# PSUM banks for the early up tiles and the gate map of a PEER layer: a second tag for every other tile

## The chip, the cores and the metric

The kernel runs on one core of one Trainium2 chip. The metric is the device time of one execution in microseconds, from three runs of the kernel before, and one further execution that the hardware profiler recorded. The engines are TensorE (PE in the rows, its weight loads PEld), VectorE (DVE), ScalarE (ACT), GpSimd (POOL) and SyncE (SP, which issues most DMAs). Each has a queue of its own and works its instructions in the order in which they stand there.

## The reference, cut to what matters

One decoder layer on 1024 tokens of width 1024. Two mixers (a gated linear recurrence and a state-space scan) come first; the part that the change touches is the PEER layer behind them, a mixture of 16,384 single-neuron experts. Each token scores 2 x 128 keys for each of 8 heads, takes 16 of the 128 x 128 pairs per head, and sums gelu(h . u) times a gate times v over its 128 experts:

```python
def block(hb):
    qh = (hb @ w_q).reshape(tb, PEER_HEADS, 2, PEER_HALF)
    s1 = jnp.einsum('thd,nd->thn', qh[:, :, 0], keys1)
    s2 = jnp.einsum('thd,nd->thn', qh[:, :, 1], keys2)
    v1, i1 = lax.top_k(s1, PEER_TOPK)
    v2, i2 = lax.top_k(s2, PEER_TOPK)
...
    gates = jax.nn.softmax(best.astype(jnp.float32), axis=-1).astype(hb.dtype)
    act = jax.nn.gelu(jnp.einsum('td,thkd->thk', hb, u_tab[eidx]), approximate=False)
    return jnp.einsum('thk,thkd->td', gates * act, v_tab[eidx])
```

## The kernel before, in words

The tokens are split. For the first 384 the kernel gathers the rows of u and v that each token needs, one indirect DMA of 128 rows (one per token) at a time (`gather`, L957; dot products on VectorE at L982, weighted sums at L998). For the other 640 (`ND`) it computes densely: for each of 128 groups of 128 experts (a group is called an expert e in the code, and here) it multiplies the tile of u with all 640 tokens, applies GELU, multiplies with a map of gates, and multiplies the result with v.

The stage that the change touches stands between the mixers and the dense loop. It holds three things at once.

- `choose` (L895 to L951) on VectorE picks the experts of four blocks of 128 tokens.
- `gate_map` (L1011 to L1060) turns the picks of a block into a dense map, in steps of 8 tokens, 16 steps to a block, 80 in all. A step makes three one-hot tiles on VectorE (`oB` L1043, `oA` L1044, `oH` L1045), eight products `oL` on ScalarE (L1047), sixteen 128x128 matmuls on TensorE (L1051, L1052) into two PSUM tiles `pg` of four tokens each, and two copies of each tile on ScalarE (`Gs`, L1054). Both `pg` tiles have the tag `s5`, with two banks. The products `oL` and the one-hot tiles have three buffers each. The maps go to DRAM (`gd`, L1060).
- The early up tiles (L1352 to L1355): for 64 of the 128 experts the up product is made ahead of the dense loop and stored in DRAM (`sd`). `up` (L1076) loads 512 KB of u as two `raw` tiles, splits each into a high and a low part (`wload`, L308: a cast on ScalarE at L255, a subtraction on VectorE at L256), and makes two halves of 320 tokens. A half is 24 matmuls of 128x320 (L1087) into one PSUM tile with the tag `mm`, two banks, and a GELU on ScalarE (L1089).

PSUM has eight banks, and the kernel gives two to each of four tags: `mm`, `hg`, `s5` and `tr`. Before this stage `hg` holds tiles of the recurrence's heads and `tr` holds transposes; in the stage `tr` is used for the three transposes at the head of each gate-map block (L1026). In the dense loop the tags `hg`, `s5` and `tr` hold the sums over v (`banks`, L1111).

The order of work on each engine is not the order of the code. The program is built with a scheduler (the flag `schedule_with_timeline_sim` at the end of the file), which takes an instruction when its inputs and its buffer are free by its own model of the chip, and writes one fixed order for each engine. So the number of banks enters the order itself. The gathers on POOL are tied to marks: `gather` may not be issued before a certain weight split or matmul of the stage (L961 to L967).

Of the kernel before, what the change touches and what calls it, by code (L numbers as in the profile page):

```python
# [10 lines left out]
F32 = mybir.dt.float32  # L11
# [11 lines left out]
P = 128  # L23
# [3 lines left out]
BANK = 512  # L27
# [7 lines left out]
NSB = ND // 2  # L35
# [54 lines left out]
def hymba_kernel(  # L90
# [26 lines left out]
    def T(pool, shape, dt, tag, bufs=None):  # L117
        return pool.tile(shape, dt, name=f"{tag}_{next(cnt)}", tag=tag, bufs=bufs)
# [5 lines left out]
    def bc(ap, axis, n):  # L124
        a = ap.unsqueeze(axis)
        shape = list(a.shape)
        shape[axis] = n
        return a.to_broadcast(shape)
# [7 lines left out]
    ps = ctx.enter_context(tc.tile_pool(name="ps", bufs=2, space=bass.MemoryType.PSUM))  # L136
# [171 lines left out]
    def wload(src, nk):  # L308
        res = []
        for k0 in range(0, nk, KH):  # L310
            raw = T(wp, [P, KH * P], F32, "raw", bufs=NRAW)
            nc.sync.dma_start(raw, src[:, k0 * P : (k0 + KH) * P])
            w2 = T(wp, [P, 2, KH * P], F32R, "w2", bufs=NW2)
            marks[phase[0]].append(split(w2[:, 0, :], w2[:, 1, :], raw))
            res.append(w2)
        return res
# [694 lines left out]
    def gate_map(gm, blk):  # L1011
        ei = T(gm, [P, HK], I32, "dei")
        nc.sync.dma_start(ei, eid[blk])
        gf = T(gm, [P, HK], F32, "dgt")
        nc.sync.dma_start(gf, gtd[blk])
        sel = []
        for n, (op, c) in enumerate(((ALU.logical_shift_right, 7), (ALU.bitwise_and, NK - 1))):
            t = T(gm, [P, HK], I32, "seli")
            TS(t, ei, c, None, op)
            tf = T(gm, [P, HK], F32, f"self{n}")  # L1020
            nc.vector.tensor_copy(tf, t)
            sel.append(tf)
        sel.append(gf)
        pt = T(ps, [P, BANK], F32, "tr", bufs=2)
        for n, t in enumerate(sel):
            nc.tensor.transpose(pt[:, n * P : (n + 1) * P], t, ident)  # L1026
        sT = T(gm, [P, 3, P], F16, "selT", bufs=2)
        nc.scalar.copy(sT[:, 0:2, :], pt[:, 0 : 2 * P].rearrange("p (n t) -> p n t", n=2))
        gs = T(gm, [P, P], F32, "gsel")
        nc.scalar.mul(gs, pt[:, 2 * P : 3 * P], GSC)  # L1030
        nc.scalar.copy(sT[:, 2, :], gs)
        sL = T(gm, [P, P], F32, "self0")
        TT(sL, gs, sT[:, 2, :], ALU.subtract)  # L1033
        for g in range(P // TG):
            gq = [T(gm, [P, NI, TG], F32, "Gs", bufs=4) for _ in range(2)]
            for o8 in range(0, TG, OT):
                t8 = g * TG + o8
                col = lambda n: bc(sT[:, n, t8 : t8 + OT].rearrange("p (q r) -> p q r", r=2), 2, P)
                one = lambda tag: T(gm, [P, OT // 2, P, 2], F16, tag, bufs=3)
                A, B, Ah = one("oA"), one("oB"), one("oH")  # L1040
                Al = T(gm, [P, OT, P], F16, "oL", bufs=3)
                at = lambda t, i: t[:, i // 2, :, i % 2]
                TT(B, iotar, col(1), ALU.is_equal)  # L1043
                TT(A, iotar, col(0), ALU.is_equal)  # L1044
                TT(Ah, A, col(2), ALU.mult)  # L1045
                for i in range(OT):
                    nc.scalar.mul(Al[:, i], at(A, i), sL[:, t8 + i : t8 + i + 1])  # L1047
                for o4 in range(0, OT, 4):
                    pg = T(ps, [P, 4, P], F32, "s5", bufs=2)
                    for i in range(o4, o4 + 4):  # L1050
                        nc.tensor.matmul(pg[:, i - o4, :], at(B, i), at(Ah, i), start=True, stop=False)  # L1051
                        nc.tensor.matmul(pg[:, i - o4, :], at(B, i), Al[:, i], start=False, stop=True)  # L1052
                    for c in range(2):
                        nc.scalar.mul(  # L1054
                            gq[c][:, :, o8 + o4 : o8 + o4 + 4],
                            pg[:, :, c * NI : (c + 1) * NI].rearrange("p t i -> p i t"),
                            1.0 / GSC,
                        )
            for c in range(2):
                nc.sync.dma_start(gd[(blk * P - T0D) // TG + g, :, c * NI : (c + 1) * NI, :], gq[c])  # L1060

    def dense_in(du, gm):
        h2T = []
        for k in range(KD):
            t = T(du, [P, 2, ND], F32R, "h2T", bufs=KD)
            r = T(gm, [P, ND], F32, "S", bufs=3)
            nc.scalar.dma_start(r, h2s[k])
            split(t[:, 0, :], t[:, 1, :], r)
            h2T.append(t)
        return h2T  # L1070
# [2 lines left out]

    early = [i * NK // SPN for i in range(SPN)]

    def up(h2T, e, g):  # L1076

        w2 = wload(u_t[e], KD)
        for sb in range(2):
            cs_ = slice(sb * NSB, (sb + 1) * NSB)  # L1080
            pt = T(ps, [P, BANK], F32, "mm", bufs=2)[:, :NSB]
            n = 0
            for k in range(KD):
                wk = w2[k // KH]
                kc = slice((k % KH) * P, (k % KH + 1) * P)
                for i, j in ((0, 0), (0, 1), (1, 0)):
                    nc.tensor.matmul(pt, wk[:, i, kc], h2T[k][:, j, cs_], start=(n == 0), stop=(n == 3 * KD - 1))  # L1087
                    n += 1
            ACT(g[:, cs_], pt, AF.Gelu)  # L1089

    def dense(dp, dq, h2T):
# [4 lines left out]
        def gate(e):  # L1096
            if e % IG == 0:
                gtile[0] = T(dq, [P, NTG, IG, TG], F32, "gt", bufs=2)
                nc.sync.dma_start(gtile[0], gd[:, :, e : e + IG, :].rearrange("n p i t -> p n i t"))
            g = T(dp, [P, ND], F32, "S", bufs=NS)  # L1100
            if e in early:
                nc.sync.dma_start(g, sd[early.index(e)])
            else:
                up(h2T, e, g)
            gv = g.rearrange("p (n t) -> p n t", t=TG)
            TT(gv, gv, gtile[0][:, :, e % IG, :], ALU.mult)  # L1106
            w = ws[e] = T(dp, [P, 2, ND], F32R, "W", bufs=NW)
            split(w[:, 0, :], w[:, 1, :], g)
# [234 lines left out]
    h2T = dense_in(du, gm)  # L1343
# [6 lines left out]
    for blk in range(T0D // P, S // P):  # L1350
        gate_map(gm, blk)
    for n, e in enumerate(early):  # L1352
        g = T(gm, [P, ND], F32, "S", bufs=3)
        up(h2T, e, g)
        nc.sync.dma_start(sd[n], g)  # L1355
    phase[0] = "dense"
    gmx.close()
# [91 lines left out]
```

## Time and profile before

| | us |
|---|---|
| three runs: lowest, median, highest | 2968.72, 2981.1, 2986.83 |
| the profiled execution | 2974.75 |
| its span, first to last instruction | 2973.0 |

The granted TensorE clock of the profiled execution was 0.976 of full on average. In the rows, a line number is that of the kernel before; an entry such as `mm<-h2T,w` names the tile written and the tiles read, with buffer numbers left out, and the tag `s5` appears as `s`. Busy time is the time in which an engine works on at least one instruction. Matmuls overlap in the pipeline, so the mean duration of one is longer than the distance between two starts.

### The profile page before, as it was taken

How to read it: one execution, taken by the hardware profiler on the slowest of the kernel's cores; microseconds unless marked ns; L12 is line 12 of the kernel's file. 1: busy time of each engine (PE TensorE's matmuls, PEld its weight loads, DVE VectorE, ACT ScalarE, POOL GpSimd, SP SyncE). 2: the span in 40 equal slices, each digit the busy share in tenths (PEclk: the TensorE clock that was granted, in tenths of full speed). 3: DMA queues.
4: the chain of work that ended last, by engine and by line, in shares of the span. 5: the costliest groups of instructions: out<-in, count | busy, mean ns of one | idle time of the engine just before them, and what ended most of it. 6: DMA issues, size and time to landing. Idle time of an engine off the chain costs nothing.

```text
span 2973.0 us, 46130 instructions
## 1 busy us (share of the span) xinstructions
PE 2782.4 (94%) x16071; PEld 2492.3 (84%) x16071; DVE 2464.2 (83%) x5598; ACT 1093.4 (37%) x2405; POOL 1143.7 (38%) x1043
## 2 busy tenths in 40 slices
PE   6899989989989799999999999999999999999995
PEld 5777978778878799989998888888888888888874
DVE  7869745977799999998568888978888888888988
ACT  3224431423310688979423322222222222222222
POOL 1765100231222002333344554545555556445552
PEclk9899989999999999999999999999999999999997
DMA  9822334686766358999999999989999899999986
GB/s 335 267 82 68 109 117 160 223 286 194 250 226 191 120 195 306 349 337 358 363 340 364 327 312 330 334 310 342 348 343 335 299 337 319 322 324 321 319 302 226
DMA packets 376265, 816.69 MB, mean 275 GB/s; under 512 B 60128, under 2 KB 153952, under 8 KB 370912
## 3 DMA queue, kind: packets, MB, share of 16 engines
q0 software_dynamic: 110592, 402.70, 38.4%
q1 hardware_dynamic: 227248, 388.74, 37.7%
q10 hardware_dynamic: 38192, 22.31, 2.7%
q8 instruction: 126, 2.06, 0.3%
q14 instruction: 107, 0.88, 0.1%
HBM read 732.27 MB, written 81.36 MB: 274 GB/s over the span
## 4 chain that ended last, share of the span: by engine, by line
PE 33%; DVE 19%; issue 19%; DMA 15%; POOL 10%; ACT 4%; POOLq 0%; ACTq 0%; DVEq 0%; SPq 0%
PE mm L1087 10%; PE mm L326 10%; POOL row L957 8%; DMA row<-in_v_rows_dram,ei 7%; PE hg L1163 3%; PE s L1163 3%; PE tr L1163 2%; DVE row L982 2%; DVE acc L998 2%; DMA row<-in_u_rows_dram,ei 2%; ACT oL L1047 2%; DMA vraw<-in_v_rows_dram 2%; DMA S<-sd 1%; DVE v L256 1%; PE hg L742 1%
## 5 line engine op out<-in xcount | busy, mean ns | idle before, releaser
L1087 PE MATMUL mm<-h2T,w 128*128 128x320 f32 x6144 | 943.5, 312 | 37.0 <-ACT S L1089 26.2
L1087 PEld LDWEIGHTS mm<-h2T,w 128*128 128x128 f32 x6144 | 913.9, 189 | 47.6 <-ACT S L1089 31.3
L957 POOL DMA_INDIRECT row<-in_u_rows_dram,ei x384 | 455.5, 1186 | 1148.9 <-DVE dots L982 648.1
L957 POOL DMA_INDIRECT row<-in_v_rows_dram,ei x384 | 523.2, 1363 | 486.5 <-DVE acc L998 400.4
L326 PE MATMUL mm<-hT,w 128*128 128x256 f32 x2304 | 529.4, 384 | 3.8 <-ACT tmp L610 2.6
L998 DVE SCALAR_TENSOR_TENSOR acc<-row,dots,acc 128x1024 f32<-128x1024 f32 x381 | 487.7, 1280 | 44.6 <-DMA row<-in_v_rows_dram,ei 41.3
L326 PEld LDWEIGHTS mm<-hT,w 128*128 128x128 f32 x2304 | 434.1, 193 | 61.5 <-ACT tmp L610 3.0
L982 DVE CUSTOM_DVE_ANT_0 row<-row,h2n 128x1024 f32<-128x1024 f32 x384 | 462.2, 1216 | 26.5 <-DMA row<-in_u_rows_dram,ei 25.7
L1163 PE MATMUL hg<-v,W 128*128 128x512 f32 x1296 | 352.5, 394 | 13.9 <-DVE v L256 5.5
L1163 PE MATMUL s<-v,W 128*128 128x512 f32 x1296 | 347.4, 391 | 2.2 <-DVE dacc L1176 1.1
L255 ACT CAST v<-vraw 128x512 fp32r<-128x512 f32 x256 | 158.5, 620 | 514.1 <-DMA vraw<-in_v_rows_dram 268.2
L1163 PE MATMUL tr<-v,W 128*128 128x512 f32 x1248 | 338.2, 392 | 8.4 <-DVE dacc L1176 4.2
L1163 PEld LDWEIGHTS hg<-v,W 128*128 128x128 f32 x1296 | 244.4, 190 | 69.5 <-DVE v L256 8.7
L1163 PEld LDWEIGHTS s<-v,W 128*128 128x128 f32 x1296 | 242.6, 188 | 55.4 <-DVE dacc L1176 2.8
L1163 PEld LDWEIGHTS tr<-v,W 128*128 128x128 f32 x1248 | 234.5, 189 | 59.7 <-DVE dacc L1176 5.5
L256 DVE TENSOR_TENSOR v<-vraw,v 128x512 fp32r<-128x512 f32 x256 | 175.4, 686 | 88.9 <-ACT v L255 87.0
L256 DVE TENSOR_TENSOR w<-raw,w 128x512 fp32r<-128x512 f32 x256 | 175.3, 686 | 70.5 <-ACT w L255 64.5
L255 ACT CAST w<-raw 128x512 fp32r<-128x512 f32 x256 | 158.2, 621 | 172.8 <-PE mm L1087 159.1
L1047 ACT ACTIVATE oL<-oA,self 128x128 f16<-128x128 f16 x640 | 196.3, 414 | 4.6 <-DVE self L1033 3.9
L1089 ACT ACTIVATE S<-mm 128x320 f32<-128x320 f32 x256 | 109.3, 439 | 206.3 <-PE mm L1087 165.2
L255 ACT CAST W<-S 128x640 fp32r<-128x640 f32 x128 | 93.1, 729 | 216.9 <-PE s L1163 65.1
L1106 DVE TENSOR_TENSOR S<-S,gt 128x640 f32<-128x640 f32 x128 | 104.1, 818 | 39.8 <-DMA S<-sd 37.6
(375 smaller groups left out, 3140.1 us busy)
## 6 DMA issues: line engine op xcount, KB each, us to landing
raw<-in_u_t_dram SPq DMA_DIRECT2D x256, 256.0 KB
vraw<-in_v_rows_dram SPq DMA_DIRECT2D x256, 256.0 KB
gd<-Gs SPq DMA_DIRECT2D x40, 1024.0 KB
gt<-gd SPq DMA_DIRECT2D x32, 1280.0 KB
w<-in_w_in_dram SPq DMA_DIRECT2D x56, 512.0 KB
w<-in_w_q_dram SPq DMA_DIRECT2D x48, 512.0 KB
sd<-S SPq DMA_DIRECT2D x64, 320.0 KB
S<-sd SPq DMA_DIRECT2D x64, 320.0 KB
```

Of the source, the lines that this page charges most:

```text
L255: nc.scalar.copy(hi, src)
L256: return nc.vector.tensor_tensor(lo, src, hi.bitcast(F32), ALU.subtract)
L326: ins = nc.tensor.matmul(out, w[:, k * P : (k + 1) * P], rhs[k], start=(k == 0), stop=(k == nk - 1))
L742: nc.tensor.matmul(pt[:, c * half : (c + 1) * half].rearrange("p (n l) -> p n l", l=lsz), blk(lh, c), two(blk(xx, c))[:, :, 1, :], start=T ...
L957: g = nc.gpsimd.indirect_dma_start(out=t, out_offset=None, in_=table, in_offset=bass.IndirectOffsetOnAxis(ap=idx, axis=0))
L982: nc.vector.tensor_tensor_reduce(out=ut, in0=ut, in1=h2, scale=1.0, scalar=0.0, op0=ALU.mult, op1=ALU.add, accum_out=dots[:, j : j + 1],)
L998: STT(acc, vt, w[:, j : j + 1], acc, ALU.mult, ALU.add)
L1047: nc.scalar.mul(Al[:, i], at(A, i), sL[:, t8 + i : t8 + i + 1])
L1087: nc.tensor.matmul(pt, wk[:, i, kc], h2T[k][:, j, cs_], start=(n == 0), stop=(n == 3 * KD - 1))
L1089: ACT(g[:, cs_], pt, AF.Gelu)
L1106: TT(gv, gv, gtile[0][:, :, e % IG, :], ALU.mult)
L1163: nc.tensor.matmul(pv[tb], ws[e][:, a, tb * P : (tb + 1) * P], v2[:, b, :], start=(e == s and n == 0), stop=(e == s + SLAB - 1 and n == 2),)
```

## The change

The second `pg` tile of each gate-map step gets the tag `tr`, and the second half of each early up tile gets the tag `hg`. The up products inside the dense loop keep `mm` for both halves.

```diff
@@ -1046,7 +1046,7 @@
                 for o4 in range(0, OT, 4):
-                    pg = T(ps, [P, 4, P], F32, "s5", bufs=2)
+                    pg = T(ps, [P, 4, P], F32, ("s5", "tr")[o4 // 4], bufs=2)
                     for i in range(o4, o4 + 4):
@@ -1073,12 +1073,12 @@
-    def up(h2T, e, g):
+    def up(h2T, e, g, tags=("mm",)):
 
         w2 = wload(u_t[e], KD)
         for sb in range(2):
             cs_ = slice(sb * NSB, (sb + 1) * NSB)
-            pt = T(ps, [P, BANK], F32, "mm", bufs=2)[:, :NSB]
+            pt = T(ps, [P, BANK], F32, tags[sb % len(tags)], bufs=2)[:, :NSB]
@@ -1351,7 +1351,7 @@
         g = T(gm, [P, ND], F32, "S", bufs=3)
-        up(h2T, e, g)
+        up(h2T, e, g, ("mm", "hg"))
```

The scheduler writes other orders for it. In the rows below, the last number of a tile counts the tiles of the program; an early expert takes 64 of them, and the first one's `mm` tile is 11306.

On TensorE, at the last gate group of the whole gate map (the tile ending in 11282), before:

```order
L1051 LDWEIGHTS oB_11257
L1051 MATMUL s_2507_11282<-oH_11258,oB_11257 128x128
L1052 LDWEIGHTS oB_11257
L1052 MATMUL s_2507_11282<-oL_11259,oB_11257 128x128
L1087 MATMUL mm_14314<-h2T_7594,w_2839_14306 128x320 x2
L1087 MATMUL mm_14314<-h2T_7599,w_2841_14311 128x320 x3
L1087 MATMUL mm_14314<-h2T_7604,w_2841_14311 128x320 x3
L1087 MATMUL mm_14314<-h2T_7609,w_2841_14311 128x320 x3
```

And now:

```order
L1051 LDWEIGHTS oB_11257
L1051 MATMUL tr_11282<-oH_11258,oB_11257 128x128
L1052 LDWEIGHTS oB_11257
L1052 MATMUL tr_11282<-oL_11259,oB_11257 128x128
L1087 MATMUL mm_13162<-h2T_7599,w_2715_13159 128x320 x2
L1087 MATMUL hg_13188<-h2T_7599,w_2715_13159 128x320 x2
L1087 MATMUL mm_13226<-h2T_7579,w_2720_13218 128x320 x2
L1087 MATMUL hg_13252<-h2T_7579,w_2720_13218 128x320 x2
L1087 MATMUL mm_13162<-h2T_7599,w_2715_13159 128x320
L1087 MATMUL mm_13162<-h2T_7604,w_2715_13159 128x320 x3
```

The last gate group stood in the middle of tile 14314, which belongs to the 48th early expert; now it stands ahead of the larger part of tile 13162, the 30th, and four up tiles of two experts are open at once behind it. In the order of before, 2,266 of the 3,072 early up matmuls are written ahead of the last gate matmul, now 1,416.

On ScalarE, in the last block of the gate map (products `oL` and copies `Gs`; L1089 is the GELU of an up half, L255 the cast of a weight tile), before:

```order
L1047 ACTIVATE oL_11148<-oA_11145,self_2403_10685 128x128 x8
L1089 ACTIVATE S_14111<-mm_14122 128x320
L1054 ACTIVATE Gs_10991<-s_2474_11082 128x64x4
L1054 ACTIVATE Gs_10992<-s_2474_11082 128x64x4
L1054 ACTIVATE Gs_10991<-s_2475_11093 128x64x4
L1054 ACTIVATE Gs_10992<-s_2475_11093 128x64x4
L1047 ACTIVATE oL_11185<-oA_11182,self_2403_10685 128x128 x8
L1089 ACTIVATE S_14111<-mm_14148 128x320
L255 CAST w_2832_14242<-raw_14240 128x512
L1054 ACTIVATE Gs_10991<-s_2480_11119 128x64x4
L1054 ACTIVATE Gs_10992<-s_2480_11119 128x64x4
```

And now:

```order
L1047 ACTIVATE oL_11148<-oA_11145,self_2403_10685 128x128 x2
L1054 ACTIVATE Gs_10991<-tr_11093 128x64x4
L1054 ACTIVATE Gs_10992<-tr_11093 128x64x4
L1047 ACTIVATE oL_11148<-oA_11145,self_2403_10685 128x128 x4
L1054 ACTIVATE Gs_10991<-s_2480_11119 128x64x4
L1054 ACTIVATE Gs_10992<-s_2480_11119 128x64x4
L1047 ACTIVATE oL_11148<-oA_11145,self_2403_10685 128x128 x2
L1047 ACTIVATE oL_11185<-oA_11182,self_2403_10685 128x128 x2
L1054 ACTIVATE Gs_10991<-tr_11130 128x64x4
L1054 ACTIVATE Gs_10992<-tr_11130 128x64x4
L1047 ACTIVATE oL_11185<-oA_11182,self_2403_10685 128x128 x4
```

Between two steps stood a GELU or a cast or both; in this place now there is neither, and copies and products follow each other alone. Ahead of the last copy `Gs` the order of before has 93 casts of weight tiles and 94 GELUs, now 59 and 58; products and copies are 640 and 320 in both.

On VectorE, at the same steps (L1043 to L1045 are the one-hot passes, L982 a dot of a gathered row in two instructions, L256 the split of a weight tile), before:

```order
L1044 TENSOR_TENSOR oA_11182<-iotar_7619,selT_10680 128x1024
L1045 TENSOR_TENSOR oH_11106<-oA_11104,selT_10680 128x1024
L1043 TENSOR_TENSOR oB_11105<-iotar_7619,selT_10680 128x1024
L982 ISA row_26234,dots_26080<-row_26234,h2n_26078 128x1024
L982 ISA dots_26080 128x1
L1044 TENSOR_TENSOR oA_11219<-iotar_7619,selT_10680 128x1024
L256 TENSOR_TENSOR w_2825_14178<-raw_14176,w_2825_14178 128x512
L1045 TENSOR_TENSOR oH_11147<-oA_11145,selT_10680 128x1024
L1043 TENSOR_TENSOR oB_11146<-iotar_7619,selT_10680 128x1024
L256 TENSOR_TENSOR w_2827_14183<-raw_14181,w_2827_14183 128x512
L982 ISA row_26237,dots_26080<-row_26237,h2n_26078 128x1024
L982 ISA dots_26080 128x1
```

And now:

```order
L1045 TENSOR_TENSOR oH_11147<-oA_11145,selT_10680 128x1024
L1044 TENSOR_TENSOR oA_11182<-iotar_7619,selT_10680 128x1024
L1043 TENSOR_TENSOR oB_11183<-iotar_7619,selT_10680 128x1024
L1045 TENSOR_TENSOR oH_11184<-oA_11182,selT_10680 128x1024
L1044 TENSOR_TENSOR oA_11219<-iotar_7619,selT_10680 128x1024
L1043 TENSOR_TENSOR oB_11220<-iotar_7619,selT_10680 128x1024
L1045 TENSOR_TENSOR oH_11221<-oA_11219,selT_10680 128x1024
L1044 TENSOR_TENSOR oA_11256<-iotar_7619,selT_10680 128x1024
L1043 TENSOR_TENSOR oB_11257<-iotar_7619,selT_10680 128x1024
L1045 TENSOR_TENSOR oH_11258<-oA_11256,selT_10680 128x1024
L256 TENSOR_TENSOR w_2715_13159<-raw_13157,w_2715_13159 128x512
L256 TENSOR_TENSOR w_2720_13218<-raw_13216,w_2720_13218 128x512
```

Dots and splits stood between the one-hot passes of these steps; now the passes stand alone to the last one, and the splits of the next up tiles follow behind. Ahead of the last product `oH` the order of before has 87 dots and 90 splits since the first one-hot pass, now 45 and 55. The order on POOL is the same in both.

## Rows read from the trace of the kernel before

**Rows 1.** The head of the page.
```profile
span 2973.0 us, 46130 instructions
```

**Rows 2.** Two lines: ns min/median/max, first and last start us, forms.
```profile
L1054 ACT ACTIVATE Gs<-s x320: 364/391/461, 1007.0 to 1441.5; 128x256 f32<-128x256 f32 x160
...
L1355 SPq DMA_DIRECT2D sd<-S x64: 319/327/4293, 1023.9 to 1561.0; - x64
```

**Rows 3.** Stretches: us, busy (x) of PE, PEld, DVE, ACT, POOL, PEclk, DMA, GB/s.
```profile
994.00:1442.00 448.00, 422.94 (x3566) 410.72 (x3567) 416.25 (x1079) 380.95 (x1182) 108.34 (x91) 0.98 0.80 292
1442.00:1561.00 119.00, 118.42 (x805) 117.84 (x805) 73.60 (x121) 33.69 (x69) 51.34 (x44) 1.00 0.98 348
1561.00:2860.00 1299.00, 1271.45 (x6619) 1119.31 (x6618) 1106.26 (x1438) 355.55 (x633) 671.65 (x504) 0.99 0.94 329
```

**Rows 4.** Waits of PE, 900 to 1660 us: us in total, times, longest.
```profile
PE mm L1087 <- ACT S L1089: 12.6, 9, 2.5
...
PE s L1051 <- ACT Gs L1054: 3.3, 4, 1.6
```

**Rows 5.** L1087 behind the gate map: us, PE busy (x), clock, DMA.
```profile
1442.00:1561.00 119.00, 118.42 (x805) 1.00 0.98 348
```

**Rows 6.** Timeline of PE, one step: start us, us, what.
```profile
1013.29 0.22 PE L1051 MATMUL s<-oH,oB 128*128 128x128 f16 x1
...
1014.15 0.22 PE L1052 MATMUL s<-oL,oB 128*128 128x128 f16 x1
```

**Rows 7.** Timeline of ACT, from 1199.92 us.
```profile
1199.92 1.19 ACT L1054 ACTIVATE Gs<-s 128x256 f32<-128x256 f32 x4
1200.99 2.47 ACT L1047 ACTIVATE oL<-oA,self 128x128 f16<-128x128 f16 x8
1203.33 0.44 ACT L1089 ACTIVATE S<-mm 128x320 f32<-128x320 f32 x1
1203.65 0.64 ACT L255 CAST w<-raw 128x512 fp32r<-128x512 f32 x1
1204.16 1.21 ACT L1054 ACTIVATE Gs<-s 128x256 f32<-128x256 f32 x4
```

**Rows 8.** Groups of ACT, 994 to 1442 us: xcount | busy us, mean ns.
```profile
L255 ACT CAST w<-raw 128x512 fp32r<-128x512 f32 x94 | 58.6, 627 | 11.5 <-DMA raw<-in_u_t_dram 4.9 <-PE mm L1087 3.4 <-DVE dgt L940 1.8
L1089 ACT ACTIVATE S<-mm 128x320 f32<-128x320 f32 x94 | 41.5, 445 | 26.7 <-PE mm L1087 23.8 <-issue 2.6
L1089 ACT ACT_TABLE_LOAD x5 | 6.4, 1283 | 0.1
...
L941 ACT ACT_TABLE_LOAD x4 | 5.1, 1283 | 0.1
```

**Rows 9.** Timeline of DVE, from 1288.39 us.
```profile
1288.39 1.22 DVE L982 CUSTOM_DVE_ANT_0 row<-row,h2n 128x1024 f32<-128x1024 f32 x1
1289.54 0.08 DVE L982 DVE_READ_ACCUMULATOR2_ANT dots<- 128x1 f32 x1
1289.54 0.68 DVE L1045 TENSOR_TENSOR oH<-oA,selT 128x1024 f16<-128x1024 f16 x1
1290.14 0.68 DVE L256 TENSOR_TENSOR w<-raw,w 128x512 fp32r<-128x512 f32 x1
1290.74 0.98 DVE L930 TENSOR_TENSOR oh<-posf,ranks 128x800 f32<-128x800 f16 x1
```

**Rows 10.** Short stretches at the first ups, columns as in rows 3.
```profile
985.00:995.00 10.00, 8.46 (x47) 7.08 (x45) 9.93 (x52) 3.46 (x8) 1.12 (x2) 1.00 0.45 131
995.00:1000.00 5.00, 0.52 (x2) 0.52 (x3) 5.00 (x11) 1.59 (x6) 0.00 (x0) 0.75 0.17 52
...
1015.00:1020.00 5.00, 2.46 (x18) 1.93 (x18) 5.00 (x34) 5.00 (x18) 0.00 (x0) 1.00 0.00 0
```

**Rows 11.** Timeline of PE, from 1000.18 us.
```profile
1000.18 2.87 PE L1087 MATMUL mm<-h2T,w 128*128 128x320 f32 x10
1002.86 0.33 PE L1051 MATMUL s<-oH,oB 128*128 128x128 f16 x1
```

## The prediction

> **What bounds the kernel now.** I read the head of the page first: the span is 2973.0 us [rows 1]. The profiled execution took 2974.75 us, so 1.75 us lie around the span; it is 6 us under the median of the three runs (2981.1), and I carry a difference found in the trace over to that median as it stands. Next I looked for the marks of the stage that the change touches: its first matmuls stand at about 994 us, the last gate-map copy out of PSUM (L1054) starts at 1441.5 and the last store of an early up tile (L1355) is issued at 1561.0 [rows 2]. The table of stretches cut at these marks is the main view [rows 3]. From 994 to 1442 three engines are nearly full: TensorE 422.9 of 448 us, VectorE 416.3, ScalarE 381.0. From 1442 to 1561, with only early up tiles left, TensorE alone is full (118.4 of 119 us), the other two have slack. After 1561 TensorE is at 98% (1271 of 1299 us) almost to the end. So what this stage loses or gains moves the end one for one, and the reader should see how little idle TensorE time there is to win anywhere.
>
> The waits of TensorE from 900 to 1660 us say it in numbers: 12.6 us for the GELU that frees an `mm` bank (L1089) and 3.3 us for the copy that frees an `s5` bank (L1054) [rows 4]. These 15.9 us are all its waits for a bank.
>
> **The change part by part.** No instruction is added or removed: the same 3,072 early up matmuls, 1,280 gate-map matmuls, copies and DMAs are there. Two things change. First, the banks: each up half now waits for its own pair (`mm` or `hg`), each gate group for `s5` or `tr`. `hg` and `tr` have other users before 994 us and in the dense stage after 1561; inside the stage `tr` is shared only with 12 transposes (L1026). A removed bank wait is worth between 0 and 15.9 us. Second, and this decides, the scheduler that writes the engines' orders now sees four up banks and four gate banks, and it pulls the gate map forward. Counted in the two orders of TensorE, the last gate group stands behind 2,266 of the 3,072 up matmuls before, and behind 1,416 now. Each engine works its order in turn, so the ups written behind the last gate group can't fill time ahead of it.
>
> Prices on TensorE. From 1442 to 1561, 805 up matmuls took 118.42 us, 0.147 us each [rows 5]. The sixteen gate matmuls of one step (8 tokens) start 0.86 us apart from first to last, 0.0573 each [rows 6]. Up to the last gate group that makes 2266 x 0.147 + 1280 x 0.0573 = 333 + 73 = 406 us before, and 1416 x 0.147 + 73 = 281 us now.
>
> Prices on ScalarE, as distances between the starts of neighbours [rows 7]: four gate copies 1.07 us, eight `oL` products 2.34, one GELU 0.32, one weight cast 0.51. A step of the gate map thus costs ScalarE 2.34 + 1.07 = 3.41 us, and 80 of them 273 us, wherever they stand. It was busy 381.0 us up to 1442 [rows 3], with 94 casts and 94 GELUs in it [rows 8]. In the order ahead of the last gate copy stood 93 casts and 94 GELUs, now 59 and 58: 34 x 0.51 + 36 x 0.32 = 29 us move behind it, 352 us stay.
>
> Prices on VectorE [rows 9]: a dot of a gathered row 1.15 us start to start, a one-hot pass 0.60, a weight split 0.60. It was busy 416.3 us up to 1442 [rows 3]. Ahead of its last one-hot product the new order has 55 splits instead of 90 and 45 dots instead of 87: 35 x 0.60 + 42 x 1.15 = 69 us less, 347 us stay.
>
> So the balance is gone. Before, up to the last gate group: 406 us TensorE, 416 VectorE, 381 ScalarE. Now: 281, 347, 352. ScalarE and VectorE set the end of the gate map, and TensorE waits in its order for `oL`; behind each waiting gate matmul stand the ups that used to fill this time. It is worst in the last 32 steps, where 355 ups (7.4 experts) stand now: 355 x 0.147 + 512 x 0.0573 = 82 us of TensorE against 32 x 3.41 + 15 x 0.83 = 122 us of ScalarE (15 halves, each with a cast and a GELU).
>
> How full do the leading engines get? Before, the two fullest reached 423 / 448 = 94% and 416 / 448 = 93%, ScalarE 85%. I take 94%, since the leader now is the fullest: 352 / 0.94 = 374 us, so the gate map ends at about 994 + 374 = 1368 (1442 before). Then 1,656 ups remain at 0.147 us: 243.6 us. VectorE and the DMA engines have as much to do there as they had between 1442 and 1561: the order puts 85 dots into it, 41 in 119 us, where 42 stood before, at a DMA share of 0.98 [rows 3]. The early tiles end at 1368 + 244 = 1612 instead of 1561: +51 us. The removed bank waits are in this already, since TensorE's own work is no longer the limit ahead of 1368. The dense stage has the same counts and keeps its length. Sum: 2974.75 + 51 = 3026 us for an execution like the profiled one, 2981 + 51 = 3032 us on the median; I say 3031.
>
> The ends of the unknown, how full ScalarE gets: at 100% of its busy time the gate map ends at 1346 and the loss is 29 us. Summed from start-to-start prices alone, 640 x 0.293 + 320 x 0.268 + 58 x 0.32 + 59 x 0.51 and about 20 us for the nine table loads at 1.28 [rows 8] and the small copies, it has 342 us to do, and the loss is 19 us. At the 85% that it had before it is 352 / 0.85 = 414 us and a loss of 91 us. 94% is nearest to the rows of the engines that led.
>
> **The rivals.** *Not slower, because the bank waits were the limit.* Four banks let TensorE run on while ScalarE is late, the 15.9 us go, and the moved gate map costs nothing: 2981 - 16 = 2965 us. For it: these waits are in the trace [rows 4]. Against it: it holds only if the gate map is done by 1561 - 244 = 1317 us, 352 us of ScalarE work in 323. Every price of ScalarE would have to fall by 8%. The Trainium skill (Perfetto Trace Analysis, section Optimizing Tensor Performance, Matmuls) says that independent groups of matmuls should rotate through different PSUM banks, so that one group's evacuation overlaps the next group's matmuls. By that rule this rival would win; the trace agrees that there are such waits, but shows no more than 15.9 us of them.
>
> *The clock falls.* Where TensorE waited for the activations, its granted clock fell to 0.75 of full (995 to 1000 us, 0.52 of 5 us busy), from 1.00 in the 10 us before, of which it was busy 8.46 [rows 10]; the ten ups from 1000.18 to 1002.86 us then took 0.27 us each [rows 11], twice their price at 2.4 GHz less a little, so the low level, 1.2 GHz. If the idle that I forecast holds the clock there through the last 32 steps, TensorE needs 355 x 0.27 + 512 x 0.115 (twice 0.0573) = 155 us, against ScalarE's 122: another 33 us, 3064 us. Against it: from 1015 to 1020 us TensorE was busy 2.46 of 5 us and had a clock of 1.00 [rows 10]. The Trainium skill (TensorE: Matmul & The Clock Gate, section A second HAM failure mode: psum-queue depth-cycling) tells of a kernel that cycles through PSUM banks and idles so briefly and often between groups that its clock swings between the two levels; the trace agrees that some us of idling can bring the low one.
>
> *A gather-bound tail.* In VectorE's new order no dot stands in the last ten steps of the gate map, 34 us at 3.41. If the gathers of that time have to be made up behind it, where DMA is as full as it was from 1442 to 1561, the dots and not the ups set the tail: 34 us more, 3065 us. Against it: the 85 dots counted above hold these already, and the gathers' own order on POOL is unchanged.
>
> **How the numbers follow.** My forecast gets 0.73, no loss 0.12 (0.03 of it faster by over 1%, which no sum here reaches), the clock 0.08, the tail 0.07. Of the forecast, 0.05 lies at full filling, under 30 us. About 1%, 30 us, is what a measurement of this kernel can tell from no change. So faster has 0.03, within 1% 0.09 + 0.05 = 0.14, slower 0.68 + 0.08 + 0.07 = 0.83. The range goes from the start-to-start sum, 2981 + 19 = 3000, to just over the clock and the tail, 3066; the 91 us end and the case without loss stay outside.
>
> **What would show it.** Right: the last gate copy starts near 1368 us and the last early store is issued near 1612; TensorE idles some 40 us in the last 32 steps of the gate map, for `oL` or for gate copies; ScalarE is over 90% busy there; waits for L1089 nearly vanish; the dense stage is 1412 us long as before. Wrong: a gate map that ends by 1320 us, or TensorE as full up to its end as before while its order is the one counted above. Then ScalarE's price or its filling is not what I took.

## The result, and the profile after

The change makes the kernel slower: 3048.06 us median of 5 runs (3041.06 to 3054.6) beside 2978.88 for the kernel before in the same comparison, a ratio of 1.0233 with a 95% interval from 1.0213 to 1.0252. That is 69 us where 50 were forecast; the time lies inside the range.

The profiled execution of the changed kernel took 3054.6 us, the slowest of the five. The head of its page, and the marks of the stage (columns as in [rows 2], with the copies now in two lines, one per bank):

```profile
span 3052.8 us, 46161 instructions
```

```profile
L1054 ACT ACTIVATE Gs<-s x160: 360/428/692, 1006.0 to 1377.5; 128x256 f32<-128x256 f32 x160
L1054 ACT ACTIVATE Gs<-tr x160: 361/438/694, 1006.5 to 1378.0; 128x256 f32<-128x256 f32 x160
L1355 SPq DMA_DIRECT2D sd<-S x64: 319/326/8030, 1031.1 to 1621.7; - x64
```

The gate map's last copy starts at 1378.0 (forecast 1368; before 1441.5), the last early store is issued at 1621.7 (forecast 1612; before 1561.0). So of the 79.8 us between the two spans, 60.7 lie ahead of the last early store and 19.1 behind it.

The table of stretches, cut at the new marks, with the columns of [rows 3]:

```profile
994.00:1378.00 384.00, 342.70 (x2713) 309.51 (x2714) 340.27 (x949) 344.96 (x1108) 54.03 (x45) 0.88 0.65 238
1378.00:1622.00 244.00, 244.00 (x1656) 243.98 (x1655) 150.48 (x251) 68.93 (x142) 107.85 (x90) 0.99 0.95 332
1622.00:2940.00 1318.00, 1272.38 (x6562) 1121.16 (x6561) 1104.02 (x1431) 353.35 (x629) 666.16 (x504) 0.98 0.92 322
```

The first line is the loss. TensorE had 1416 x 0.147 + 73 = 281 us of work up to 1378 by the prediction's prices, in 384 us: 103 us lost. Before it was 406 us in 448: 42 lost. The difference is the 61 us. The second line answers to [rows 5]: 1,656 ups in 244.00 us, 0.147 each, TensorE full, as forecast. ScalarE's 345 and VectorE's 340 us in the first line are the work that was counted for them (342 to 352 and 347).

The first line hides two parts. Cut where the last 32 steps of the gate map begin, the changed kernel has:

```profile
994.00:1256.00 262.00, 238.54 (x1941) 227.14 (x1942) 254.41 (x804) 229.35 (x714) 32.30 (x28) 0.93 0.64 233
1256.00:1378.00 122.00, 104.16 (x774) 82.38 (x774) 85.86 (x146) 115.61 (x395) 21.73 (x18) 0.77 0.69 249
```

and the kernel before, in the same first stretch and then up to its own end of the gate map:

```profile
994.00:1256.00 262.00, 242.76 (x2029) 235.18 (x2030) 253.52 (x799) 229.12 (x701) 42.86 (x36) 0.97 0.69 251
1256.00:1442.00 186.00, 180.18 (x1539) 175.54 (x1539) 162.74 (x281) 151.83 (x482) 65.48 (x56) 1.00 0.95 350
```

Up to 1256 both kernels have VectorE full, at 97%, but the changed one is already behind: by then TensorE has done 1,163 ups and 768 gate matmuls, for 1,287 and 736 before. At the prediction's prices that is 215 us of work for 231, so 16 of the 61 us are lost ahead of 1256. Much of it goes in two bunches of gate-map steps, at 1050 (54 gate matmuls and no up) and at 1120; the kernel before has TensorE busy in both stretches for the whole time:

```profile
1050.00:1062.00 12.00, 6.80 (x54) 4.77 (x52) 12.00 (x45) 11.97 (x40) 0.00 (x0) 0.78 0.46 186
1120.00:1135.00 15.00, 10.21 (x98) 8.77 (x97) 15.00 (x70) 15.00 (x52) 0.00 (x0) 0.89 0.62 250
```

The other 45 us are lost behind 1256: before, three engines share 186 us; after, ScalarE alone is full (115.6 of 122 us, 95%) and TensorE does what little stands ahead of the last gate group. The groups of TensorE from 1256 to 1378 (count, busy us, mean ns; then the idle time ahead of them) say how little:

```profile
L1087 PE MATMUL mm<-h2T,w 128*128 128x320 f32 x125 | 27.8, 362 | 6.6 <-ACT w L255 4.1 <-DVE w L256 2.5
L1051 PE MATMUL tr<-oH,oB 128*128 128x128 f16 x128 | 27.0, 250 | 2.7 <-ACT Gs L1054 2.4 <-issue 0.3
L1087 PE MATMUL hg<-h2T,w 128*128 128x320 f32 x134 | 26.4, 336 | 0.0
L1051 PE MATMUL s<-oH,oB 128*128 128x128 f16 x128 | 25.9, 246 | 4.6 <-ACT Gs L1054 2.8 <-ACT oL L1047 1.7
L1052 PE MATMUL tr<-oL,oB 128*128 128x128 f16 x128 | 25.7, 238 | 2.0 <-ACT oL L1047 0.9
L1052 PE MATMUL s<-oL,oB 128*128 128x128 f16 x128 | 24.9, 234 | 1.0
```

All 512 matmuls of 32 steps, and 259 ups: 512 x 0.0573 + 259 x 0.147 = 67 us of work in 122. Only 18 us of the missing 55 show as idle; the rest hides in the busy time. A part of that is the clock: at the granted 0.77 of the mean, 67 us would take some 87, an estimate by proportion. The rest is that the records of matmuls that start apart still join up, as here, where a new pair starts about every 0.29 us, ScalarE's price of one product `oL`:

```profile
1363.39 0.27 PE L1052 MATMUL tr<-oL,oB 128*128 128x128 f16 x1
1363.45 0.31 PE L1051 MATMUL tr<-oH,oB 128*128 128x128 f16 x1
1363.69 0.27 PE L1052 MATMUL tr<-oL,oB 128*128 128x128 f16 x1
```

The reader should see that "104 of 122 us busy" is not an engine that had enough to do.

The timeline of ScalarE there shows what set the pace:

```profile
1355.36 1.45 ACT L1047 ACTIVATE oL<-oA,self 128x128 f16<-128x128 f16 x4
1356.53 0.81 ACT L1054 ACTIVATE Gs<-s 128x256 f32<-128x256 f32 x2
1357.06 1.46 ACT L1047 ACTIVATE oL<-oA,self 128x128 f16<-128x128 f16 x4
1358.22 0.82 ACT L1054 ACTIVATE Gs<-tr 128x256 f32<-128x256 f32 x2
1358.75 1.47 ACT L1047 ACTIVATE oL<-oA,self 128x128 f16<-128x128 f16 x4
```

No idle time, and 1358.75 - 1355.36 = 3.39 us per step of eight tokens (forecast 3.41, from the kernel before). Last, the waits of TensorE from 900 to 1720 us, beside [rows 4]:

```profile
PE s L1051 <- ACT Gs L1054: 8.5, 16, 3.1
...
PE mm L1087 <- ACT S L1089: 4.6, 2, 3.6
...
PE tr L1051 <- ACT Gs L1054: 2.9, 14, 0.3
```

The wait for L1089 fell from 12.6 to 4.6 us, as a second pair of banks should make it. Those for the gate map's copies rose from 3.3 to 11.4, with twice the banks. Together they stay at 16 us.

### The profile page after: what moved, and what is told of

Same layout as the page of the kernel before. It is cut to its first block, busy times and chain, and to the rows that moved or that the text cites. A ratio compares the mean times of both kernels' runs of the same rounds, so it can differ in the third digit from the quotient of the medians.

```text
span 3052.8 us, 46161 instructions
## 1 busy us (share of the span) xinstructions
PE 2835.0 (93%) x16071; PEld 2524.2 (83%) x16071; DVE 2465.7 (81%) x5598; ACT 1093.5 (36%) x2405; POOL 1144.1 (37%) x1043
## 4 chain that ended last, share of the span: by engine, by line
PE 26%; issue 23%; DVE 17%; DMA 14%; POOL 14%; ACT 5%; POOLq 0%; ACTq 0%; DVEq 0%; SPq 0%
POOL row L957 11%; PE mm L326 9%; DMA row<-in_v_rows_dram,ei 7%; PE mm L1087 5%; DMA vraw<-in_v_rows_dram 3%; DVE row L982 3%; ACT oL L1047 2%; PE hg L1163 2%; PE tr L1163 2%; DMA row<-in_u_rows_dram,ei 2%; PE s L1163 2%; PE hg L1087 2%; DVE acc L998 1%; ACT Gs L1054 1%; PE hg L742 1%
## 5 line engine op out<-in xcount | busy, mean ns | idle before, releaser
L1087 PE MATMUL mm<-h2T,w 128*128 128x320 f32 x4608 | 740.8, 317 | 46.5 <-ACT S L1089 29.1
L1087 PEld LDWEIGHTS mm<-h2T,w 128*128 128x128 f32 x4608 | 705.2, 193 | 57.8 <-ACT S L1089 32.7
L982 DVE CUSTOM_DVE_ANT_0 row<-row,h2n 128x1024 f32<-128x1024 f32 x384 | 462.1, 1215 | 30.1 <-DMA row<-in_u_rows_dram,ei 24.3
L255 ACT CAST v<-vraw 128x512 fp32r<-128x512 f32 x256 | 158.5, 620 | 557.2 <-DMA vraw<-in_v_rows_dram 298.6
L256 DVE TENSOR_TENSOR w<-raw,w 128x512 fp32r<-128x512 f32 x256 | 175.2, 688 | 121.7 <-ACT w L255 117.8
L1087 PE MATMUL hg<-h2T,w 128*128 128x320 f32 x1536 | 258.0, 314 | 0.0
L256 DVE TENSOR_TENSOR v<-vraw,v 128x512 fp32r<-128x512 f32 x256 | 175.2, 685 | 93.6 <-ACT v L255 87.5
L1087 PEld LDWEIGHTS hg<-h2T,w 128*128 128x128 f32 x1536 | 236.7, 192 | 0.0
L255 ACT CAST w<-raw 128x512 fp32r<-128x512 f32 x256 | 158.8, 634 | 178.4 <-PE mm L1087 137.5
L1047 ACT ACTIVATE oL<-oA,self 128x128 f16<-128x128 f16 x640 | 207.0, 465 | 3.7 <-DVE self L1033 3.7
L1089 ACT ACTIVATE S<-mm 128x320 f32<-128x320 f32 x192 | 81.8, 441 | 234.3 <-PE mm L1087 170.9
```

The lines of the kernel that those rows point to most:

```text
L255: nc.scalar.copy(hi, src)
L256: return nc.vector.tensor_tensor(lo, src, hi.bitcast(F32), ALU.subtract)
L982: nc.vector.tensor_tensor_reduce(out=ut, in0=ut, in1=h2, scale=1.0, scalar=0.0, op0=ALU.mult, op1=ALU.add, accum_out=dots[:, j : j + 1],)
```

## The experiments

The theory, called ORDER in the expectations: the loss comes from where the gate map stands among the ups in TensorE's order, since what is written behind the last gate group can't fill time ahead of it. BANK: it comes from sharing the banks `tr` and `hg`. Lengths of stretches are read from one profiled execution each, times are medians, and the brackets behind them hold the ratio to the kernel before on the same chip with its 95% interval.

**One half of the change at a time.** `gate_only` keeps the edit of the gate map, `up_only` that of the up tiles:

```diff
-                    pg = T(ps, [P, 4, P], F32, "s5", bufs=2)
+                    pg = T(ps, [P, 4, P], F32, ("s5", "tr")[o4 // 4], bufs=2)
```

```diff
-        up(h2T, e, g)
+        up(h2T, e, g, ("mm", "hg"))
```

> Only the gate map gets its second pair of banks (tr), the up tiles keep mm for both halves. In its order the last gate group stands behind 17.5 experts' up matmuls (47.2 before, 29.5 with the whole change). Theory ORDER (ScalarE and VectorE set the end of the gate map, and the ups written behind it come late): ScalarE has about 332 us up to there, at the 90% to which it was filled in the changed kernel 369 us, so the gate map ends near 1363 us; 46.5 experts at 7.06 us follow, the last early store at about 1690 us, 130 us later than before: about 3109 us, slower than the whole change. Rival BANK (the shared bank tr or hg itself costs the time, by waits on its other users): this part alone costs a share of the 69 us, so 2979 to 3048 us. Rival WAITS (more banks take bank waits away): 2963 to 2979 us.

> Only the early up tiles get hg for their second half, the gate map keeps s5 alone. In its order the last gate group stands behind 52.3 experts' up matmuls (47.2 before). Theory ORDER: the gate map is spread over more ups, TensorE is the fullest again (442 us up to the last gate group, at 94% about 470 us, gate map until 1464 us), 11.7 experts at 7.06 us follow, the last early store near 1547 us, 14 us earlier than before: 2965 us, between 2955 and 2982. Rival BANK (hg itself costs): what the gate map's part alone doesn't cost of the 69 us, 2985 to 3048 us.

`gate_only` took 3096.09 us (1.0392, 1.0352 to 1.0432), 1.6% more than the whole change, 13 us below ORDER's sum and far outside both rivals. Its marks and stretches (the first one cut at its first gate copy, 1004):

```profile
L1054 ACT ACTIVATE Gs<-tr x160: 369/462/677, 1005.2 to 1347.1; 128x256 f32<-128x256 f32 x160
L1355 SPq DMA_DIRECT2D sd<-S x64: 319/326/853, 1056.6 to 1675.3; - x64
```

```profile
1004.00:1348.00 344.00, 293.45 (x2098) 237.32 (x2098) 282.10 (x828) 312.90 (x1032) 19.20 (x16) 0.77 0.50 188
1348.00:1676.00 328.00, 328.00 (x2234) 328.00 (x2233) 206.09 (x341) 93.61 (x188) 146.77 (x123) 1.00 0.94 331
```

The gate map alone pulls forward still further when it alone has more banks: its end is at 1347, with 2,232 ups left, and these take 328 us with TensorE full. `up_only` took 2981.49 us (0.9997, 0.9979 to 1.0016): more banks for the ups push the gate map back (last copy 1471.2, last store 1553.8, 7 us earlier than before), and the total stays. So the end of the early stage follows the order in both directions. The time of `up_only` decides little: it lies at the upper edge of ORDER's range (2982) and 3.5 us under BANK's, and its early stage gained 7 us where 14 were expected. The wait for L1089 fell there from 12.6 to 4.5 us, about as much as those 7 us.

**The order without the banks.** `old_banks_early_map` has the kernel before's banks; a weight split of early expert n may not be issued before a step of the gate map that runs ahead of it:

```diff
+            cut = split(w2[:, 0, :], w2[:, 1, :], raw)
+            if hold[0] is not None:
+                issue_after(cut, hold[0])
...
+                gsteps.append(TT(Ah, A, col(2), ALU.mult))
...
+        hold[0] = gsteps[min(int(2.4 * n) + 8, 80) - 1] if n > 1 else None
```

> The banks of before for everything (mm for both halves, s5 for every group); instead the weight splits of the early up tiles are held back in the order until a set number of gate-map steps is written, so that the last gate group stands behind 31.4 experts' ups, close to the 29.5 of the changed kernel. Theory ORDER: ScalarE has 355 us up to there, at 90% 394 us, gate map until about 1388 us, 32.6 experts at 7.06 us follow: last early store near 1618 us, 57 us later than before, 3036 us (3015 to 3060), with no bank changed. Rival BANK: the time of before, 2979 us within 1%.

It took 3046.12 us (1.0231, 1.0192 to 1.0269), within ORDER's range and the loss of the change, with no bank changed. Its last copy stands at 1393.4 and its last store at 1625.6:

```profile
994.00:1394.00 400.00, 332.32 (x2806) 313.32 (x2807) 352.87 (x966) 350.91 (x1119) 59.10 (x49) 0.91 0.66 239
1394.00:1626.00 232.00, 230.47 (x1568) 229.67 (x1567) 143.02 (x239) 65.05 (x132) 103.30 (x87) 1.00 0.96 333
```

The same picture as after the change: the map 48 us earlier than before, and 1,566 ups alone behind it. So the order is sufficient for the loss.

**The banks without the order.** Four kernels write the gate map at a pace: `gate_map` yields after each step of 8 tokens, and before early expert n the steps up to a + r n are taken; the first one-hot pass of a step is issued after the last weight split so far.

```diff
-    for blk in range(T0D // P, S // P):
-        gate_map(gm, blk)
+    maps = itertools.chain.from_iterable(gate_map(gm, blk) for blk in range(T0D // P, S // P))
...
+        while done < min(10 + 1.25 * n, 80):
+            next(maps)
+            done += 1
...
+        paced[0] = marks["pre"][-1]
```

`new_banks_spread_map` has the change's banks, with a = 10 and r = 1.25 as above.

> The banks of the changed kernel for everything; instead each step of the gate map is written behind the weight split of an early expert, 10 steps ahead and then 1.25 steps to an expert, so that the last gate group stands behind 56 experts' ups (47.2 before, 29.5 with the change). Theory ORDER: TensorE is the fullest throughout, 468 us up to the last gate group, at 94% 498 us, 8 experts at 7.06 us follow: last early store near 1549 us, 12 us earlier than before, 2967 us (2950 to 2982). Rival BANK: it stays as slow as the changed kernel, 3040 to 3055 us.

It took 3007.14 us (1.0084, 1.0053 to 1.0115), and neither theory had that. Its last copy stands at 1512.1 and its last store at 1574.8, 14 us later than before; the other 19 of the 33 us between its span (3005.7) and that of the kernel before lie in the dense stage. The stretches show where TensorE lost time in the early one:

```profile
1030.00:1050.00 20.00, 19.98 (x183) 19.06 (x182) 17.53 (x91) 19.97 (x65) 0.00 (x0) 0.92 0.47 181
1050.00:1062.00 12.00, 6.70 (x48) 4.58 (x47) 12.00 (x51) 11.97 (x39) 0.00 (x0) 0.65 0.53 214
...
1120.00:1135.00 15.00, 8.88 (x73) 7.05 (x72) 15.00 (x82) 15.00 (x52) 0.00 (x0) 0.68 0.46 176
```

In the 12 us from 1050 TensorE ran 48 gate matmuls and no up, while VectorE and ScalarE were full: the ten steps taken ahead bunch the map at the stage's start, where `choose` keeps VectorE busy. From 1120 the same picture comes back, with 73 matmuls in 15 us. It is the fault of the change again, and at the same two places where the changed kernel loses its first 16 us; this kernel was a bad test of the banks. Two further paces avoid it: `new_banks_old_pace` (a = 0, r = 1.7), whose last gate group stands behind 47.0 experts' ups as before, and an even one with a = 2, r = 1.3, with the change's banks (`new_banks_even_map`) and with the old ones (`old_banks_even_map`).

> The banks of the changed kernel, and the pace of the kernel before: each step of the gate map is written behind the weight split of an early expert at 1.7 steps to an expert, so that the last gate group stands behind 47.0 experts' ups (47.2 before, 29.5 with the change), with the 8th to 72nd step within 2 experts of before. Only the banks are then new. Theory ORDER (the whole loss is the order's): the time of before or the 16 us of bank waits less, 2965 to 2990 us, last early store at 1545 to 1565 us. Rival BANK (the shared banks cost something themselves, in this stage or by the hand-over to the dense stage): above 2995 us.

> The banks of the changed kernel, and the gate map spread evenly from its first step on: 2 steps ahead and then 1.3 to an expert (16th step at 11.0 experts, last at 60.0). In the run with 10 steps ahead and 1.25 to an expert TensorE did no up matmul from 1048 to 1062 us, since 16 steps stood behind 5 experts' ups there. Theory FRONT (that bunch at the start is why it was slower than before): TensorE is now the fullest from the first step to the last, 526 us of work at 95% to 96% end at 1547 us, 2967 us (2950 to 2985). Rival TAIL (a map that ends late delays the dense stage, which reads it from DRAM): the last early store is as early, but the dense stage gets longer by 10 us or more, 2985 to 3010 us.

> The same even order (2 steps ahead, 1.3 to an expert, last gate group behind 60.0 experts' ups) with the banks of before. Theory ORDER: the banks are worth at most the 16 us of waits for them, so it lies 0 to 16 us above the run with the new banks, 2955 to 2995 us. Rival WAITS (it is the four banks that let TensorE run on): 2985 us or more, and at least 15 us above the run with the new banks.

`new_banks_old_pace` took 2996.68 us (1.0051, 1.0033 to 1.0069): 7 us above ORDER's range and inside BANK's. By its time it counts for BANK. Its profile has the last store at 1561.0, as in the kernel before, so the loss of the early stage is gone; what that execution (2985.71 us, the fastest of 12) has too much lies in its dense stage, 1423 us for 1409 to 1412. What the median has above it is in no profile. So up to 17 us may come with the banks or with the edit that sets the pace, in a way that the order of the early stage doesn't explain; the 61 us don't. A kernel with the old banks at this pace was not run, so which of the two it is stays open. `new_banks_even_map` took 2975.21 us (0.9983, 0.9967 to 0.9999), the lowest ratio of all versions, and `old_banks_even_map` 2981.97 (1.0006, 0.9986 to 1.0026); FRONT and ORDER hold, TAIL and WAITS fall. In the even kernel with the new banks the last copy comes 84 us later than before and the early tiles still end in time:

```profile
L1058 ACT ACTIVATE Gs<-tr x160: 368/404/469, 1007.4 to 1525.9; 128x256 f32<-128x256 f32 x160
L1365 SPq DMA_DIRECT2D sd<-S x64: 319/327/1524, 1030.6 to 1559.0; - x64
```

```profile
994.00:1526.00 532.00, 512.73 (x4175) 501.38 (x4174) 468.98 (x1165) 406.15 (x1230) 149.01 (x123) 0.98 0.81 296
1526.00:1559.00 33.00, 33.00 (x227) 33.00 (x227) 17.00 (x28) 7.97 (x18) 12.38 (x10) 1.00 1.05 369
```

TensorE is 96% full up to the map's end, and little stands behind it. At this pace the change's banks come out some 7 us faster (2981.97 - 2975.21), with intervals that overlap, so a gain by the banks is not shown. But these banks can be had without the loss; it is the order that the scheduler makes of them that costs.

**The dense stage.** Its length, from the last early store to the end of the span, was forecast as unchanged and came out 19 us longer. The kernel before and the changed kernel were profiled once more, unaltered:

> The kernel before, once more with a profile. It tells how much the dense stage differs between executions of one kernel: it was 1412 us in the first profile, which lay 8 us under this kernel's median, and 1431 us in the changed kernel. If the 19 us are a spread of executions, it comes out between 1410 and 1430 here; if it is 1412 again within 2 us, the changed kernel's dense stage is truly longer.

> The changed kernel once more, unaltered, for one more look at its dense stage, which took 1431 us in its first profile (3052.8 less 1621.7) against 1412 and 1409 in the two of the kernel before. If the dense stage is truly longer behind the new order: 1424 to 1436 us, with the early stage again ending near 1621. If the first profile was a long one by chance: 1405 to 1418 us, and a span of 3027 to 3040.

The kernel before (2974.01 us; span 2972.2, last store 1562.8) has 1409.4 us there, the changed one (3046.86 us; span 3045.1, last store 1623.4) 1421.7. That lies between the two expectations, 2 us below the one that takes the stage for truly longer and 4 above the other. The early stage differs by 60.6 us in this pair too. All the profiles, in us:

| kernel | last gate group behind so many experts' ups | last copy | last store | dense stage |
|---|---|---|---|---|
| before, twice | 47.2 | 1441.5, 1443.5 | 1561.0, 1562.8 | 1412.0, 1409.4 |
| the change, twice | 29.5 | 1378.0, 1379.9 | 1621.7, 1623.4 | 1431.1, 1421.7 |
| gate_only | 17.5 | 1347.1 | 1675.3 | 1421.2 |
| up_only | 52.3 | 1471.2 | 1553.8 | 1425.7 |
| old_banks_early_map | 31.4 | 1393.4 | 1625.6 | 1411.5 |
| new_banks_spread_map | 56 | 1512.1 | 1574.8 | 1430.9 |
| new_banks_old_pace | 47.0 | 1434.9 | 1561.0 | 1422.9 |
| new_banks_even_map | 60.0 | 1525.9 | 1559.0 | 1413.6 |
| old_banks_even_map | 60.0 | 1522.5 | 1552.2 | 1426.7 |

The work in it is nearly the same everywhere. It takes 1409 to 1431 us, and neither the banks nor the end of the gate map sort these numbers cleanly: three of the four profiles with the old banks lie at 1409 to 1412, four of the five with the change's banks at 1422 to 1431, and the two even kernels are the other way round. Single profiles can't settle it, since 29 executions of the kernel before alone lie between 2968.98 and 2994.74 us. If the early stage ends in every execution where it does in the profiles, the medians leave 69 - 61 = 8 us for the dense stage, an estimate.

In the changed kernel TensorE waits more there for the GELU that frees an up bank; from the two second profiles, before (1563 to 2972 us) and after (1622 to 3045 us):

```profile
PE mm L1087 <- ACT S L1089: 12.3, 10, 2.7
```

```profile
PE mm L1087 <- ACT S L1089: 26.6, 11, 4.5
```

These are 14 us more, about as much as the 12 by which the stage is longer in this pair. But the same wait is as long in `old_banks_early_map` (1626 to 3037 us), whose dense stage is 1411.5 us, no longer than before:

```profile
PE mm L1093 <- ACT S L1095: 25.6, 9, 4.3
```

So this wait alone does not make the stage longer. Nor is it settled why ScalarE is later with these few GELUs. At one of them (about 2182 us in the first profile of the changed kernel) ScalarE's idle time of 8.3 us, with the GELU queued behind it, ended with the arrival of a tile of v:

```profile
2183.83 0.62 ACT L255 CAST v<-vraw 128x512 fp32r<-128x512 f32 x1 [8.30 <-DMA vraw<-in_v_rows_dram]
```

Whether late transfers explain the rest was not tried.

## Why the prediction was right, and where its sizes were off

**The mechanism held.** No work is added; a scheduler that sees more banks writes the gate map ahead, and the ups behind the last gate group are missing ahead of it. `old_banks_early_map` makes the loss from the order alone, and `new_banks_even_map` has the banks without the loss. The count of ups behind the last gate group gives the tail each time: 1,656 took 244.0 us, 2,232 in `gate_only` 328.

**ScalarE and VectorE as the limit: right, but not in one piece.** The prediction took ScalarE as the leader over the whole map and one filling for it, 352 us at 94%, so 374. Measured were 345 us of work in 384, 90%. The mis-sized term is that filling. Up to 1256 VectorE was the fullest, at 254 of 262 us, and ScalarE was 88% busy, just as before the change; only from there did ScalarE lead, at 95%. The leaders in turn had 254 + 116 = 370 us of work, more than any one engine's 345, and 370 in 384 is 96%. So the early stage lost 61 us instead of 51.

That the last 32 steps took 122 us, ScalarE's sum in the text, is luck in part. The 355 ups counted for them begin behind the last matmul of the 48th step, at 1240 us, and from there to the map's end it took 138 us. In the first 16 of these TensorE was full with 107 of the ups, and ScalarE was busy for 11 of 17 us; only the rest, with 249 ups ahead of the last gate matmul, fits the 122.

**TensorE's idle time of some 40 us in those steps:** by work it was 55, but only 18 show as idle; the rest stands in the records as busy time.

**The dense stage "keeps its length":** off by 19 us in the first pair of profiles and 12 in the second, and by some 8 on the medians (69 less the 61 of the early stage). No step of the prediction had a price for it, and its cause is open. That the time still lies in the range is not this forecast's merit alone: the range was drawn up to 3066 for the clock and the tail, and both fell.

**No loss through the banks:** fell. The waits that it counts on did shrink, from 12.6 to 4.6 us for L1089, but the map ended at 1378, not by 1317. The Trainium skill (Perfetto Trace Analysis, section Optimizing Tensor Performance, Matmuls) advises to rotate independent groups of matmuls through different PSUM banks; the trace agrees in those 8 us, though the waits for the gate map's copies rose by as much, and in the changed kernel as scheduled the measurement decides against it, 1.0233.

**The clock:** it did fall, and the price wasn't paid. The short stretches around the end of the gate map, columns as in [rows 3]:

```profile
1340.00:1360.00 20.00, 16.61 (x95) 9.29 (x93) 11.37 (x18) 20.00 (x73) 0.00 (x0) 0.59 0.62 255
1360.00:1379.00 19.00, 16.58 (x84) 10.71 (x84) 6.97 (x11) 18.68 (x63) 0.00 (x0) 0.50 0.35 136
1379.00:1400.00 21.00, 21.00 (x139) 21.00 (x138) 10.78 (x19) 5.82 (x12) 7.26 (x6) 0.95 1.02 339
```

A granted clock of 0.50 is the low level, 1.2 GHz. But there are almost only gate matmuls in these steps, 16 x 0.115 = 1.8 us of them by the rival's price for that level, in a step that takes ScalarE 3.39. The rival charged 355 ups at the low level to 122 us; 107 of them ran ahead at a clock of 1.00 (1240 to 1256 us), and over the 122 us the clock was 0.77 on average. What ScalarE waited for TensorE in these 122 us bounds the price, 2.8 + 3.2 = 6.0 us, whatever made TensorE late:

```profile
L1054 ACT ACTIVATE Gs<-s 128x256 f32<-128x256 f32 x64 | 23.3, 462 | 2.8 <-PE s L1052 2.8
...
L1089 ACT ACTIVATE S<-mm 128x320 f32<-128x320 f32 x5 | 2.2, 445 | 3.2 <-PE mm L1087 3.2
```

In the 21 us behind the map, with ups alone, the clock was 0.95 on average.

**The gather-bound tail:** fell. TensorE was full from 1378 to 1622 (244.00 of 244.00 us), with a DMA share of 0.95.

## What to carry to other kernels

Where a scheduler writes the order, the number of buffers is an input to the order, and more of them for one of two interleaved jobs lets that job run ahead: count, in the new order, the work of each engine up to the last instruction of the job that moved, and what stands behind it. Do that sum stretch by stretch, with the leader of each stretch, and not once for the whole: a bunch at the start of the stage cost time here as well as the one at its end. If the extra buffers are wanted all the same, fix the pace of the interleaving along with them; here that turned a loss of 2.3% into a time within 0.2% of the kernel before.

## What the runs showed of the hardware that was not expected

TensorE's busy time can look full when it has little to do. From 1360 to 1370 us it was busy 8.74 of 10 us with 48 gate matmuls, 0.18 us each, while the same matmuls start 0.0573 us apart at full clock [rows 6]:

```profile
1360.00:1370.00 10.00, 8.74 (x48) 4.95 (x48) 3.79 (x6) 10.00 (x37) 0.00 (x0) 0.50 0.37 153
```

The low clock (0.50) is one part of that: at twice 0.0573 they would fill 5.5 us, an estimate. The other part is that a record here lasts 0.27 to 0.31 us, as long as ScalarE's 0.29 for the product that each pair waits for. The count of matmuls times their price tells how much there was to do; the busy share does not.

And the low clock cost next to nothing here, where another engine set the pace: ScalarE's step took 3.39 us at that clock, and 3.41 by its prices in the kernel before [rows 7].
